# Wide GpSimd work of a hybrid backbone's mixers moved to VectorE and ScalarE

## The chip, the cores and the metric

One core of a Trainium2 chip. The metric is the device time of one execution in microseconds (us); the kernel before takes 3044.57 us, the median of three runs (3042.0 to 3048.34). TensorE (PE in the profile) multiplies matrices, VectorE (DVE) and ScalarE (ACT) work on tiles in SBUF and on PE's results in PSUM, GpSimd (POOL) works on SBUF alone, and SyncE (SP) issues the DMAs.

## The reference, cut to what matters

Two layers over 512 latent tokens and 256 context tokens of width 1024. A layer projects the modulated tokens, runs three token mixers, merges them with sigmoid gates, projects, normalises, and ends in a SwiGLU feed-forward:

```python
px = _split_in(h_x @ lp['w_in'])                       # all inputs of the mixers
p  = softmax(einsum(q, k) * MLA_SCALE); y_mla = p @ v  # 8 heads, 768 keys for latent queries
f  = lb + (1 - lb) * sigmoid(z); k = (1 - lb) * sigmoid(-z)   # gates of the recurrence, 4 heads,
S_t = diag(f_t) S_{t-1} + k_t v_t^T;  o_t = S_t^T q_t         # forwards and backwards
y_diff = rms((softmax(q1 k1) - lam * softmax(q2 k2)) @ v)     # 4 heads, rotary on q and k
m  = sum_i sigmoid(h @ w_gate[i] + b_gate[i]) * (y[i] @ w_branch[i]);  y = m @ w_o
```

Everything is fp32; the result is the latent stream.

## The kernel before, in words

All large products are made in three passes on rounded halves: a weight tile `wr` is rounded to a high part `wh` (`split_w`, line 380), the remainder is its low part `wl`, and a product is high x high + high x low + low x high (`mm3`). Activations are split likewise (`split`). Tile names in the profile are these names: `h` the modulated tokens, `k` a ring of eight large tiles of the mixers, `s` a ring of 768-wide slabs, `b` and `S` banks of PSUM, `sm` small columns.

Two kinds of work are woven into one fixed instruction order at build time. A list of jobs (projections, gates, branches, output projection, feed-forward; one weight tile each) is the filler; the mixers run as generators beside it, one after the other: attention (`mla`, 48 query tiles in layer 0 and 32 in layer 1), differential attention (`diff`), the recurrence (`hgrn`). The class `Clock` (line 93) keeps a forecast of when each engine comes free and when each tile is ready; `note` (line 199) has a duration for each kind of instruction, and for instructions of VectorE and GpSimd on SBUF it also keeps the two from overlapping (`port`, line 171). A mixer yields `At(t)`, and `weave` (line 461) then emits filler until the forecast of TensorE reaches t. A plain `yield` is a point at which the differential attention's preparation of the next head (`prep_qk`, line 1190) lets the current head go on. At run time the engines only follow their queues; a wrong forecast is a wait.

Where the weight parts are made: `split_w` gives the high part to GpSimd in the mixer stages when its forecast is more than a microsecond ahead of ScalarE's, else to ScalarE; the low part goes to the engine that the job names (`Job.eng`; "gpsimd" for the input projections, gates and branches), except that in the recurrence `lo_eng` may choose VectorE. Further GpSimd work: the softmax normalising of attention (`sB2`, line 1079, one 768- or 256-wide multiply a query tile), two rotary products a head (`prep_qk`), the rotary sum of the query projections, the scalings of the recurrence's gates in layer 1, its key sum, output gate and, on each of seven levels a head, the decay of the keys (`gen`, line 1392), and the running sum over branches (`merge_jobs`, line 1561). The recurrence's level is a chain: keys decayed, copied by ScalarE (`kcopy`), multiplied by TensorE with the queries, the queries then decayed by VectorE for the next level, and the product copied under a mask.

Small powers, the sums of the second layer's modulation weights and the affine step of the layer norms are on GpSimd too, and are not touched. Every engine call goes through the helper class `Port`, so all profile lines say L106; work is told apart by tile names and shapes.

Of the kernel before, what the change touches and what calls it, by code (L numbers as in the profile page):

```python
# [260 lines left out]
class Job:  # L261
    def __init__(self, body, load=None, n=0, eng="vector", cost=0.0):
        self.body, self.load, self.n, self.eng, self.cost = body, load, n, eng, cost
        self.raw = self.hi = self.lo = None
        self.defer = self.late = False
        self.conv = None
        self.hold = False


class Kern:  # L270
# [108 lines left out]

    def split_w(self, hi, lo, raw, eng=None):  # L380
        nc = self.nc
        if self.kp is not None and not self.inhg and self.ck.at["gpsimd"] + 1.0 < self.ck.at["scalar"]:
            nc.gpsimd.tensor_scalar(hi, raw, 1.0, 1.0, ALU.mult, ALU.mult)
        else:
            nc.scalar.copy(hi, raw)
        (eng or nc.vector).tensor_tensor(lo, raw, hi.bitcast(F32), ALU.subtract)

    def lo_eng(self, j):
        if self.inhg and j.eng == "gpsimd" and self.ck.at["vector"] < self.ck.at["gpsimd"] + 1.0:
            return self.nc.vector  # L390
        return getattr(self.nc, j.eng)

    def do_conv(self, upto):
        self.pump()
        while self.wconv < min(upto, len(self.wjobs)):
# [13 lines left out]
            j.lo = self.ck.ring("wl", 3, self.wp.tile([P, D], F32R, tag="wl", bufs=3, name=self.nm("wl")))  # L409
            self.split_w(j.hi[:, :j.n], j.lo[:, :j.n], j.raw[:, :j.n], self.lo_eng(j))  # L410
            self.rawout[j.rk] -= 1
# [506 lines left out]
    def uq_jobs(self, l):  # L918
# [4 lines left out]
        for half in range(2):  # L923
# [10 lines left out]
            def body(job, half=half):  # L934
# [3 lines left out]
                for hh in range(4):  # L938
# [59 lines left out]
    def win_jobs(self, l, names):  # L998
# [3 lines left out]
        for nmj, j in names:  # L1002
# [6 lines left out]
            def body(job, nmj=nmj, j=j, groups=groups, park=park, ctxn=ctxn):  # L1009
# [10 lines left out]
                self.done.add(f"win{l}_{nmj}{j}")  # L1020
            self.add(Job(body, self.load_fm(w, NK), 1024, "gpsimd", 24 * sum(mmcost(g[1]) for g in groups)))


    def mla(self, l):
# [54 lines left out]
        def sB2(i):  # L1079
# [91 lines left out]
    def diff(self, l):  # L1171
# [19 lines left out]
        def prep_qk(h):  # L1191
            rq, rqs, rk, rks, rv = st["raw", h]
            nc.gpsimd.tensor_tensor(rqs[:, XO:], rqs[:, XO:], rope[1][:, :TX], ALU.mult)
            yield
            nc.gpsimd.tensor_tensor(rks[:, XO:], rks[:, XO:], rope[1][:, :TX], ALU.mult)
            yield
            for rr, rs in ((rq, rqs), (rk, rks)):
                nc.vector.tensor_tensor(rr[:, XO:], rr[:, XO:], rope[0][:, :TX], ALU.mult)
                nc.vector.tensor_tensor(rr[:, XO:], rr[:, XO:], rs[:, XO:], ALU.add)
                yield  # L1200
# [13 lines left out]
            v2 = self.k6([P, 6, 256], F32R)  # L1214
            for g, m in ((0, 4), (4, 2)):
                ps = self.bank()
                for j in range(m):
# [3 lines left out]
                nc.vector.tensor_tensor(v2[:, g:g + m, P:], pv, v2[:, g:g + m, 0:P].bitcast(F32), ALU.subtract)  # L1221
                yield
            st["v", h] = v2
# [97 lines left out]
        yield At(ck.ready(*[r[:, o0:] for r in st["raw", 0]], *rope))  # L1321
        for _ in prep_qk(0):
            yield 1.0
        yield At(ck.ready(*[x[:, :, o0:] for x in st["qk", 0][:2]], st["v", 0]))
        n = len(tiles)
        per = n // 4
        pg = None
        for i in range(n + 3):
            if i < n:
# [7 lines left out]
                sB(i, 0)  # L1337
                if pg is not None:
                    next(pg, None)
                yield At(ck.freed(SS[1][:, :T]))  # L1340
                sA(i, 1)
                sB(i, 1)
                if pg is not None:
                    next(pg, None)
            elif i == n:
                sB3(i - 1)
            if 1 <= i <= n:
# [3 lines left out]
                if i < n and (i == 1 or i > 1 and i % per == 0) and h + 1 < 4:  # L1351
                    pg = prep_qk(h + 1)
                if i < n and pg is not None:
                    next(pg, None)
            if i >= 2:
# [11 lines left out]
            if i < n and i % per == per - 1 and pg is not None:  # L1367
                for _ in pg:
                    pass
                pg = None  # L1370
# [7 lines left out]
    def hgrn(self, l):  # L1378
# [13 lines left out]
        def gen(h):  # L1392
            r = st.pop(("raw", h))
            KK, QQ, TT = self.k6([P, 2, T]), self.k6([P, 2, T]), self.k6([P, 2, T])
            for d, nmj in enumerate(("ff", "fb")):
                nc.scalar.activation(TT[:, d], r[nmj][:], AF.Sigmoid)
                nc.scalar.activation(KK[:, d], r[nmj][:], AF.Sigmoid, scale=-1.0)
                if l > 0:
                    lb, l1 = self.lb[:, d, h:h + 1], self.lb1[:, d, h:h + 1]
                    nc.gpsimd.tensor_scalar(TT[:, d], TT[:, d], l1, lb, ALU.mult, ALU.add)  # L1400
                    nc.gpsimd.tensor_scalar(KK[:, d], KK[:, d], l1, 1.0, ALU.mult, ALU.mult)
            q = r["hq"]
            sq = self.slab()
# [37 lines left out]
            for lv in range(NLEV):  # L1441
# [119 lines left out]
    def merge_jobs(self, l, br, seq):  # L1561
# [30 lines left out]
        for o in range(8):  # L1592
            def gate(job, o=o):
# [8 lines left out]
            jg = Job(gate, self.load_fm(I["w_gate"][l, br][:, o * P:(o + 1) * P], NK), 1024, "gpsimd", 24 * sum(mmcost(g[1]) for g in groups))  # L1602
            gates.append(jg)

            def bran(job, o=o):
# [24 lines left out]
                if o == 7:  # L1630
                    st.clear()
                    self.done.add(f"m{l}_{seq}")
            brans.append(Job(bran, self.load_fm(I["w_branch"][l, br][:, o * P:(o + 1) * P], 4), 512, "gpsimd", 12 * sum(mmcost(g[1]) for g in groups)))
        lag = (6, 2, 8)[seq]
# [7 lines left out]
    def sweep_jobs(self, key, w, nk, tiles, lhs, use_s, needs=(), keep=2):  # L1642
# [4 lines left out]
        for k in range(nk):  # L1647
# [3 lines left out]
            def body(job, k=k):  # L1651
# [26 lines left out]
                held.clear()  # L1678
            jb = Job(body, load, 1024, "vector")
            jb.late = k >= 3  # L1680
# [369 lines left out]
```

## Time and profile before

| | |
|---|---|
| median of 3 runs | 3044.57 us |
| the profiled execution, its span | 3047.58 us, 3045.8 us |
| mean granted TensorE clock | 0.961 |
| instructions | 39105 |
| DMA | 359.14 MB, mean 118 GB/s |

The span runs from the first instruction to the last. A busy TensorE isn't TensorE at its peak, as its matmuls are pipelined; its idle time, and what ended it, says more. Idle time of an engine that nothing waits for costs nothing.

### The profile page before, as it was taken

The page shows a single profiled execution, that of the slowest core. Times are in us where ns is not written, and L with a number is a line of the kernel's source. Part 1 is how long each engine was busy: PE and PEld are TensorE (multiplying, and loading weights), DVE is VectorE, ACT ScalarE, POOL GpSimd, SP SyncE. Part 2 cuts the span into 40 slices and gives each one's busy share as a digit, 9 for nine tenths or more (in the row PEclk, how much of TensorE's full clock was granted, in tenths as well). Part 3 has the DMA queues.
Part 4 walks back from the last instruction along what each step waited for, and adds up shares of the span by engine and source line. Part 5 has one row for each costly group of instructions (what it writes and reads, how often), then busy time and mean ns, then how long its engine had stood idle before and what let it go on. Part 6 is the DMA issues. An engine that isn't in the chain of part 4 may idle for free. (4 is left out here: it accounts for less than half of the span.)

```text
span 3045.8 us, 39105 instructions
## 1 busy us (share of the span) xinstructions
PE 2772.9 (91%) x14899; PEld 2334.8 (77%) x14899; DVE 1659.1 (54%) x2398; ACT 1149.8 (38%) x2199; POOL 1001.7 (33%) x697
## 2 busy tenths in 40 slices
PE   6999987898999996999999899999899996799997
PEld 3888866777788885888888677888778775688875
DVE  4456566666773147555533765555656664622235
ACT  3544434444332124343422445443544332322222
POOL 1333332234554424333310224444336663300002
PEclk8999998999999997999999999999899997899998
DMA  6432343333333254344432354324324432433331
GB/s 212 108 102 80 111 129 93 105 115 123 115 130 116 92 178 144 121 149 132 136 128 94 120 158 130 91 77 126 102 85 149 129 110 85 140 97 97 104 131 69
DMA packets 345523, 359.14 MB, mean 118 GB/s; under 512 B 31114, under 2 KB 263044, under 8 KB 345336
## 3 DMA queue, kind: packets, MB, share of 16 engines
q1 hardware_dynamic: 343144, 351.84, 36.7%
q10 hardware_dynamic: 1680, 4.42, 0.4%
q8 instruction: 117, 1.92, 0.3%
q14 instruction: 70, 0.57, 0.1%
q0 software_dynamic: 512, 0.39, 0.1%
HBM read 298.10 MB, written 58.49 MB: 117 GB/s over the span
## 5 line engine op out<-in xcount | busy, mean ns | idle before, releaser
L106 PE MATMUL b<-h,wh 128*128 128x512 f32 (+1 forms) x5152 | 1375.2, 356 | 38.4 <-ACT h L106 16.7
L106 PEld LDWEIGHTS b<-h,wh 128*128 128x128 f32 x5152 | 909.2, 193 | 168.0 <-ACT h L106 17.9
L106 PE MATMUL b<-h,wl 128*128 128x512 f32 (+1 forms) x2576 | 907.1, 352 | 0.5 <-DVE wl L106 0.5
L106 DVE TENSOR_TENSOR wl<-wr,wh 128x1024 fp32r<-128x1024 f32 (+1 forms) x238 | 336.7, 1417 | 452.5 <-ACT wh L106 450.9
L106 PEld LDWEIGHTS b<-h,wl 128*128 128x128 f32 x2576 | 494.9, 192 | 66.0 <-DVE wl L106 1.0
L106 ACT CAST wh<-wr 128x1024 fp32r<-128x1024 f32 (+1 forms) x304 | 299.0, 988 | 417.7 <-PE b L106 325.7
L106 POOL TENSOR_TENSOR sm<-sm,mhalf 128x1 f32<-128x1 f32 (+3 forms) x80 | 56.7, 709 | 1046.1 <-DVE sm L106 1034.7
L106 POOL TENSOR_TENSOR wl<-wr,wh 128x1024 fp32r<-128x1024 f32 (+1 forms) x146 | 315.0, 2158 | 251.9 <-ACT wh L106 226.6
L106 ACT ACTIVATE s<-S,sm 128x768 f32<-128x768 f32 (+1 forms) x170 | 135.2, 796 | 383.5 <-DVE sm L106 305.9
L106 POOL TENSOR_TENSOR ln<-ln,wr 128x512 f32<-128x512 f32 x84 | 119.5, 1423 | 222.5 <-issue 161.5
L106 PE MATMUL S<-wh,ac 128*128 128x512 f32 x512 | 173.7, 404 | 17.9 <-DVE ac L106 12.8
L106 PE MATMUL b<-ident,s 128*128 128x128 f32 (+3 forms) x687 | 114.8, 282 | 70.0 <-DVE s L106 31.3
L106 DVE TENSOR_TENSOR k<-b,k 128x512 fp32r<-128x512 f32 (+1 forms) x136 | 85.1, 627 | 165.4 <-ACT k L106 165.1
L106 PE MATMUL b<-k,wh 128*128 128x512 f32 (+1 forms) x576 | 160.0, 365 | 8.6 <-ACT k L106 7.2
L106 PE MATMUL S<-k,k 96*128 96x512 f32 (+2 forms) x576 | 139.7, 345 | 28.2 <-DVE k L106 27.2
L106 DVE TENSOR_REDUCE sm<-S 128x1 f32<-128x768 f32 (+1 forms) x160 | 131.7, 837 | 47.3 <-PE S L106 47.0
L106 PE MATMUL S<-k,s 128*128 128x128 f32 (+2 forms) x704 | 132.8, 313 | 25.8 <-DVE k L106 18.3
L106 PEld LDWEIGHTS b<-ident,s 128*128 128x128 f32 (+3 forms) x687 | 82.0, 145 | 93.6 <-issue 34.0
L106 DVE TENSOR_TENSOR k<-s,k 96x768 fp32r<-96x768 f32 (+7 forms) x92 | 120.0, 1323 | 46.0 <-ACT k L106 43.2
L106 POOL TENSOR_TENSOR s<-s,s 128x512 f32<-128x512 f32 (+2 forms) x88 | 115.7, 1323 | 87.2 <-DVE s L106 63.5
L106 PEld LDWEIGHTS S<-k,k 96*128 96x128 f32 (+1 forms) x576 | 101.5, 193 | 52.6 <-DVE k L106 30.8
L106 POOL TENSOR_SCALAR wh<-wr 128x1024 fp32r<-128x1024 f32 (+1 forms) x80 | 84.5, 1063 | 164.5 <-PE b L106 148.7
(184 smaller groups left out, 4233.3 us busy)
## 6 DMA issues: line engine op xcount, KB each, us to landing
wr<-in_w_ff_dram SPq DMA_DIRECT2D x154, 512.0 KB
wr<-in_w_mod_dram SPq DMA_DIRECT2D x96, 512.0 KB
d<-s SPq DMA_DIRECT2D x88, 384.0 KB
wr<-in_w_in_dram SPq DMA_DIRECT2D x64, 512.0 KB
s<-d SPq DMA_DIRECT2D x80, 384.0 KB
wr<-in_w_gate_dram SPq DMA_DIRECT2D x48, 512.0 KB
wr<-in_w_branch_dram SPq DMA_DIRECT2D x48, 256.0 KB
wr<-in_w_o_dram SPq DMA_DIRECT2D x24, 512.0 KB
```

Source lines behind the costliest of these rows:

```text
L106: return getattr(getattr(self.clock.nc, self.eng), op)(*a, **k)
```

## The change

The engine choice goes: `split_w` always uses ScalarE for the high part and VectorE for the low part, and `lo_eng`, `Job.eng` and `Job.cost` are removed. The wide GpSimd instructions of the mixers and of the merge move to VectorE one for one, the gate scalings of the recurrence to ScalarE. In `prep_qk` the two rotary products stand before their sums, and the two transposes of the values come after an `At` for a free bank; `step` passes such an `At` on to `weave`.

```diff
-    def split_w(self, hi, lo, raw, eng=None):
+    def split_w(self, hi, lo, raw):
         nc = self.nc
-        if self.kp is not None and not self.inhg and self.ck.at["gpsimd"] + 1.0 < self.ck.at["scalar"]:
-            nc.gpsimd.tensor_scalar(hi, raw, 1.0, 1.0, ALU.mult, ALU.mult)
-        else:
-            nc.scalar.copy(hi, raw)
-        (eng or nc.vector).tensor_tensor(lo, raw, hi.bitcast(F32), ALU.subtract)
+        nc.scalar.copy(hi, raw)
+        nc.vector.tensor_tensor(lo, raw, hi.bitcast(F32), ALU.subtract)
...
-                            nc.gpsimd.tensor_tensor(qs[64:96, o:o + n], qs[64:96, o:o + n], tmp[64:96, :n], ALU.add)
+                            nc.vector.tensor_tensor(qs[64:96, o:o + n], qs[64:96, o:o + n], tmp[64:96, :n], ALU.add)
...
-            nc.gpsimd.tensor_scalar(pr[:, :n], pr[:, :n], rs[:], 1.0, ALU.mult, ALU.mult)
+            nc.vector.tensor_scalar(pr[:, :n], pr[:, :n], rs[:], None, ALU.mult)
...
-            nc.gpsimd.tensor_tensor(rqs[:, XO:], rqs[:, XO:], rope[1][:, :TX], ALU.mult)
-            yield
-            nc.gpsimd.tensor_tensor(rks[:, XO:], rks[:, XO:], rope[1][:, :TX], ALU.mult)
-            yield
             for rr, rs in ((rq, rqs), (rk, rks)):
+                nc.vector.tensor_tensor(rs[:, XO:], rs[:, XO:], rope[1][:, :TX], ALU.mult)
+                yield
                 nc.vector.tensor_tensor(rr[:, XO:], rr[:, XO:], rope[0][:, :TX], ALU.mult)
...
             for g, m in ((0, 4), (4, 2)):
+                yield At(max(ck.next("b", 4), ck.ready(rv)))
                 ps = self.bank()
...
+        def step(pg):
+            r = next(pg, None) if pg is not None else None
+            if r is not None:
+                yield r
+                next(pg, None)
...
-                    nc.gpsimd.tensor_scalar(TT[:, d], TT[:, d], l1, lb, ALU.mult, ALU.add)
-                    nc.gpsimd.tensor_scalar(KK[:, d], KK[:, d], l1, 1.0, ALU.mult, ALU.mult)
+                    nc.scalar.activation(TT[:, d], TT[:, d], AF.Identity, scale=l1, bias=lb)
+                    nc.scalar.activation(KK[:, d], KK[:, d], AF.Identity, scale=l1)
...
-            nc.gpsimd.tensor_tensor(sq[:, o0:], KK[:, 0, o0:], KK[:, 1, o0:], ALU.add)
+            nc.vector.tensor_tensor(sq[:, o0:], KK[:, 0, o0:], KK[:, 1, o0:], ALU.add)
...
-            nc.gpsimd.tensor_tensor(g[:, o0:], g[:, o0:], sg[:, o0:], ALU.mult)
+            nc.vector.tensor_tensor(g[:, o0:], g[:, o0:], sg[:, o0:], ALU.mult)
...
-                nc.gpsimd.tensor_tensor(kv, kv, tk, ALU.mult)
+                nc.vector.tensor_tensor(kv, kv, tk, ALU.mult)
...
-                        nc.gpsimd.tensor_tensor(sg[:, oo:oo + n], sg[:, oo:oo + n], mo[:, oo:oo + n], ALU.add)
+                        nc.vector.tensor_tensor(sg[:, oo:oo + n], sg[:, oo:oo + n], mo[:, oo:oo + n], ALU.add)
```

## Rows read from the trace of the kernel before

**Rows 1.** The page: busy us, share of the span, instructions of each engine.
```profile
PE 2772.9 (91%) x14899; PEld 2334.8 (77%) x14899; DVE 1659.1 (54%) x2398; ACT 1149.8 (38%) x2199; POOL 1001.7 (33%) x697
```
**Rows 2.** Windows: length, PE, PEld, DVE, ACT, POOL busy, granted clock, DMA.
```profile
126.00:384.00 258.00, 248.28 (x1539) 216.12 (x1538) 146.14 (x272) 119.28 (x271) 101.56 (x87) 0.99 0.35 108
384.00:684.00 300.00, 249.92 (x1420) 208.54 (x1419) 196.09 (x337) 130.37 (x306) 91.66 (x73) 0.93 0.36 110
684.00:912.00 228.00, 210.23 (x1326) 182.47 (x1325) 167.96 (x202) 93.14 (x163) 112.67 (x55) 0.98 0.38 123
912.00:1076.00 164.00, 161.77 (x971) 143.13 (x971) 42.97 (x66) 33.96 (x60) 77.96 (x59) 1.00 0.33 105
...
1880.00:2084.00 204.00, 198.31 (x1250) 177.35 (x1250) 98.44 (x177) 83.03 (x179) 82.38 (x63) 1.00 0.34 100
2084.00:2270.00 186.00, 162.35 (x908) 139.69 (x907) 120.91 (x207) 87.46 (x199) 66.85 (x47) 0.94 0.31 93
2270.00:2510.00 240.00, 228.03 (x1187) 190.71 (x1187) 158.00 (x197) 92.11 (x170) 146.79 (x89) 0.99 0.42 132
2510.00:2590.00 80.00, 52.46 (x229) 41.49 (x229) 36.80 (x65) 17.89 (x36) 31.79 (x22) 0.79 0.26 87
```
**Rows 3.** Waits of PE, 384 to 684: total us, times, longest us.
```profile
PE b L106 <- DVE s L106: 16.8, 6, 7.3
PE b L106 <- DVE sm L106: 10.4, 6, 2.9
PE b L106 <- ACT s L106: 7.0, 7, 2.4
PE S L106 <- ACT s L106: 6.8, 9, 1.2
PE b L106 <- DVE k L106: 4.9, 2, 2.7
PE S L106 <- DVE k L106: 4.0, 1, 4.0
```
**Rows 4.** Timeline, 393 to 403: start us, us, instruction [idle before, releaser].
```profile
397.14 2.65 POOL L106 TENSOR_TENSOR wl<-wr,wh 128x1024 fp32r<-128x1024 f32 x1
397.52 3.09 DVE L106 SCALAR_TENSOR_TENSOR s<-s,k 64x768 fp32r<-64x768 f32 x1
...
400.63 0.95 DVE L106 TENSOR_TENSOR k<-s,k 64x768 fp32r<-64x768 f32 x1
...
402.10 0.69 PE L106 MATMUL b<-ident,s 128*128 128x128 f32 x2 [7.35 <-DVE s L106]
```
**Rows 5.** Tile wl: duration ns min/median/max, first and last start, forms.
```profile
L106 DVE TENSOR_TENSOR wl<-wr,wh x238: 693/1226/3399, 6.8 to 3009.2; 128x1024 fp32r<-128x1024 f32 x117, 128x512 fp32r<-128x512 f32 x2
...
L106 POOL TENSOR_TENSOR wl<-wr,wh x146: 1262/2387/3471, 50.2 to 2581.2; 128x1024 fp32r<-128x1024 f32 x104, 128x512 fp32r<-128x512 f32 x42
```
**Rows 6.** The page's costliest groups: busy us, mean ns, idle before and releaser.
```profile
L106 DVE TENSOR_TENSOR wl<-wr,wh 128x1024 fp32r<-128x1024 f32 (+1 forms) x238 | 336.7, 1417 | 452.5 <-ACT wh L106 450.9
L106 ACT CAST wh<-wr 128x1024 fp32r<-128x1024 f32 (+1 forms) x304 | 299.0, 988 | 417.7 <-PE b L106 325.7
L106 POOL TENSOR_TENSOR s<-s,s 128x512 f32<-128x512 f32 (+2 forms) x88 | 115.7, 1323 | 87.2 <-DVE s L106 63.5
L106 POOL TENSOR_SCALAR wh<-wr 128x1024 fp32r<-128x1024 f32 (+1 forms) x80 | 84.5, 1063 | 164.5 <-PE b L106 148.7
```
**Rows 7.** Groups by line, GpSimd: the keys' decay and the normalising.
```profile
L106 POOL TENSOR_TENSOR k<-k,k 128x768 f32<-128x768 f32 x32 | 70.0, 2186 | 16.3 <-ACT s L106 8.5 <-DVE k L106 5.6 <-PE S L106 2.1
...
L106 POOL TENSOR_SCALAR s<-s,sm 128x768 f32<-128x768 f32 (+1 forms) x80 | 65.7, 822 | 203.3 <-DVE sm L106 121.7 <-issue 33.9 <-ACT s L106 16.9
```
**Rows 8.** Tile ln on DVE: a multiply by columns, min/median/max ns.
```profile
L106 DVE TENSOR_SCALAR ln<-ln,sm,sm x16: 803/807/2911, 1137.7 to 2654.1; 128x1024 f32<-128x1024 f32 x16
```
**Rows 9.** Waits of PE, 126 to 384.
```profile
PE S L106 <- DVE k L106: 8.2, 8, 1.9
```
**Rows 10.** Waits of PE, 2510 to 2590.
```profile
PE S L106 <- DVE k L106: 6.4, 2, 5.5
```

More of the change, by code (lines that the diff above doesn't have):

```diff
@@ L261, with __init__ @@
 class Job:
-    def __init__(self, body, load=None, n=0, eng="vector", cost=0.0):
-        self.body, self.load, self.n, self.eng, self.cost = body, load, n, eng, cost
+    def __init__(self, body, load=None, n=0):
+        self.body, self.load, self.n = body, load, n
         self.raw = self.hi = self.lo = None
@@ L378, in pump @@
             self.wload += 1
-    def split_w(self, hi, lo, raw, eng=None):
+    def split_w(self, hi, lo, raw):
         nc = self.nc
-        if self.kp is not None and not self.inhg and self.ck.at["gpsimd"] + 1.0 < self.ck.at["scalar"]:
-            nc.gpsimd.tensor_scalar(hi, raw, 1.0, 1.0, ALU.mult, ALU.mult)
-        else:
-            nc.scalar.copy(hi, raw)
-        (eng or nc.vector).tensor_tensor(lo, raw, hi.bitcast(F32), ALU.subtract)
[L388 to L391, printed above, removed]
+        nc.scalar.copy(hi, raw)
+        nc.vector.tensor_tensor(lo, raw, hi.bitcast(F32), ALU.subtract)
     def do_conv(self, upto):
@@ L409, in do_conv @@
             j.lo = self.ck.ring("wl", 3, self.wp.tile([P, D], F32R, tag="wl", bufs=3, name=self.nm("wl")))
-            self.split_w(j.hi[:, :j.n], j.lo[:, :j.n], j.raw[:, :j.n], self.lo_eng(j))
+            self.split_w(j.hi[:, :j.n], j.lo[:, :j.n], j.raw[:, :j.n])
             self.rawout[j.rk] -= 1
@@ L1020, in body @@
                 self.done.add(f"win{l}_{nmj}{j}")
-            self.add(Job(body, self.load_fm(w, NK), 1024, "gpsimd", 24 * sum(mmcost(g[1]) for g in groups)))
+            self.add(Job(body, self.load_fm(w, NK), 1024))
     def mla(self, l):
@@ L1221, in prep_qk @@
                 nc.vector.tensor_tensor(v2[:, g:g + m, P:], pv, v2[:, g:g + m, 0:P].bitcast(F32), ALU.subtract)
-                yield
+                if g == 0:
+                    yield
             st["v", h] = v2
@@ L1321, in diff @@
         yield At(ck.ready(*[r[:, o0:] for r in st["raw", 0]], *rope))
-        for _ in prep_qk(0):
-            yield 1.0
+        for r in prep_qk(0):
+            yield r or 1.0
         yield At(ck.ready(*[x[:, :, o0:] for x in st["qk", 0][:2]], st["v", 0]))
+        def step(pg):
[3 more added lines that the diff above has]
+                next(pg, None)
         n = len(tiles)
@@ L1337, in diff @@
                 sB(i, 0)
-                if pg is not None:
-                    next(pg, None)
+                yield from step(pg)
                 yield At(ck.freed(SS[1][:, :T]))
@@ L1342, in diff @@
                 sB(i, 1)
-                if pg is not None:
-                    next(pg, None)
+                yield from step(pg)
             elif i == n:
@@ L1352, in diff @@
                     pg = prep_qk(h + 1)
-                if i < n and pg is not None:
-                    next(pg, None)
+                yield from step(pg)
             if i >= 2:
@@ L1367, in diff @@
             if i < n and i % per == per - 1 and pg is not None:
-                for _ in pg:
-                    pass
+                for r in pg:
+                    if r is not None:
+                        yield r
                 pg = None
@@ L1601, in gate @@
                     yield c
-            jg = Job(gate, self.load_fm(I["w_gate"][l, br][:, o * P:(o + 1) * P], NK), 1024, "gpsimd", 24 * sum(mmcost(g[1]) for g in groups))
+            jg = Job(gate, self.load_fm(I["w_gate"][l, br][:, o * P:(o + 1) * P], NK), 1024)
             gates.append(jg)
@@ L1632, in bran @@
                     self.done.add(f"m{l}_{seq}")
-            brans.append(Job(bran, self.load_fm(I["w_branch"][l, br][:, o * P:(o + 1) * P], 4), 512, "gpsimd", 12 * sum(mmcost(g[1]) for g in groups)))
+            brans.append(Job(bran, self.load_fm(I["w_branch"][l, br][:, o * P:(o + 1) * P], 4), 512))
         lag = (6, 2, 8)[seq]
@@ L1678, in body @@
                 held.clear()
-            jb = Job(body, load, 1024, "vector")
+            jb = Job(body, load, 1024)
             jb.late = k >= 3
```

## The prediction

> **What bounds the kernel now.** Read the busy shares first: TensorE (PE) is busy 91% of the span, VectorE (DVE) 54%, ScalarE (ACT) 38%, GpSimd (POOL) 33% [rows 1]. A mean over stages with different limits says little, so next the windows, cut where the weight loads and parked results on SyncE change stage [rows 2]. Per row, window length less PE busy is what PE lost: attention in layer 0 (126 to 384) 9.7 us, differential attention (384 to 684) 50.1, the recurrence (684 to 912) 17.8, the rest of the merge (912 to 1076) 2.2; in layer 1 5.7 (1880 to 2084), 23.7 (2084 to 2270), 12.0 (2270 to 2510) and 27.5 (2510 to 2590). So PE's work bounds the attention stages and the merge, and waits bound the differential stages and the end of the layer 1 mixers. In those the granted clock is down too: 0.93, 0.94 and 0.79, against 0.99 to 1.00 elsewhere. As the work list is emitted in one fixed order and the layer 0 merge still runs at 99% PE busy, PE time saved earlier in layer 0 is saved at the end.
>
> Third, who ended PE's waits in the worst window [rows 3]: DVE 36.1 us (16.8 + 10.4 + 4.9 + 4.0), ACT 13.8 (7.0 + 6.8). Fourth, one such wait in order of time [rows 4]: a GpSimd low part from 397.14 to 399.79, a VectorE instruction over 64x768 that takes 3.09 us beside it, and PE standing 7.35 us until a VectorE copy queued behind that has run. The next VectorE instruction of the same width took 0.95 us at 400.63.
>
> Fifth, the price list. The same low part (1024 wide) takes VectorE 1.226 us in the median and 3.399 at worst, GpSimd 2.387 in the median [rows 5]: worst is about one GpSimd instruction more than median. The 238 on VectorE mean 1.417 [rows 6], so some 238 x 0.19 = 45 us of them are waiting for GpSimd. That is the bottleneck the change touches: not VectorE's load but what GpSimd does to it.
>
> The Trainium skill (SBUF — State Buffer, "Who interferes with whom") says that a VectorE instruction with two SBUF inputs and a GpSimd instruction that reads SBUF hold a shared port in turn, the later one blocked for the whole of the earlier. By that rule, and 3.399 against 1.226 agrees, every wide instruction that leaves GpSimd also takes a blocker away from VectorE. Were the two engines independent, the same move would only lengthen VectorE's queue, and rival A would be the outcome.
>
> **The change part by part.** (1) Low parts, 146 off GpSimd, 104 of 1024 and 42 of 512 [rows 5]: at 1.226 and 0.693 (the shortest VectorE one) 128 + 29 = 157 us go to VectorE, 315 leave GpSimd. (2) High parts, 80 off GpSimd at 1.06 us (84.5 us) to ScalarE at 0.99 [rows 6]: +79 us there; 16 scalings of the recurrence's gates go with them, at about 0.95 (three quarters of the 1024 cast as the lower end, 0.74; GpSimd's own whole microsecond as the upper): +15. (3) Softmax normalising, 80, 0.82 on GpSimd [rows 7]. VectorE's price at 768 isn't in the trace; a 1024-wide multiply by a column took 0.807 [rows 8], so 0.6 from it by width, 0.81 at most; I take 0.65 for the 64 wide and 0.3 for the 16 narrow ones: 47 us. (4) Adds and rotary products, 88, 1.32 on GpSimd [rows 6], 128x512 for the most part; half a 1.226 low part and a little: 0.65 each, 57 us. (5) The recurrence's key decay, 56 (32 are in [rows 7] at 2.19). Strided and broadcast, so nothing shows it on VectorE; by width three quarters of 1.226 is 0.92, above it at most GpSimd's 2.19. I take 1.0, nearest to the plain rows: 56 us, at the upper end 123. With 8 key sums (6 us) VectorE gets some 323 us, and gives back at least the 45 of waiting: at most 1659 + 278 = 1937 of 3046, 64%.
>
> Where do these lie? In the attention stages VectorE goes from 146 of 258 us and 98 of 204 [rows 2] up by a little over half of what GpSimd does there, to about 0.72 and 0.65 of the window. PE's only VectorE waits there are short: 8.2 us in 8 [rows 9]. A tile has 258 / 48 = 5.4 us; its normalising now stands in VectorE's queue between the reciprocal (which waits for ScalarE's exponential) and the next tile's maximum, so maximum, exponential and products of the next tile come 0.65 us later. The filler matmuls cover that; without them it would be 80 x 0.65 = 52 us. I charge a doubling of those short waits, rounded: **+10 us**.
>
> Differential attention, layer 0: the 13.8 us that ACT ends stay, ScalarE having more to do. Of DVE's 36.1 three quarters go, because low parts and casts on GpSimd stand beside the long VectorE instructions, and because the value transposes now wait, by forecast, for their bank behind filler instead of in PE's queue (the 7.35 us wait in [rows 4] is one of these; the edit adds no instruction): **-27**, bounds 0 and -50. The low clock is (1 - 0.93) x 300 = 21 us of lost full-speed work at most; half returns with the waits: **-10**, bounds 0 and -21. Layer 1, same reasoning on 23.7 us: **-12**, bounds 0 and -24, and half of 0.06 x 186 = 11 for the clock: **-5**. Recurrence, layer 0: 17.8 us, **-8**. What is late next in these stages is ScalarE: 1 us casts in front of exponentials.
>
> Recurrence and end of layer 1: 12.0 + 27.5 us. At 2510 the filler is used up and the last head's chain stands alone; 5.5 us there is one wait for a VectorE product [rows 10]. With GpSimd at 147 of 240 us in that window [rows 2] each level of the chain waits for a 2.19 us instruction and what it blocks. A decay of 1.0 us shortens a level by a microsecond or more, 28 levels, so heads use less filler and some is left for the last one. The decay's wait for ScalarE's key copy now stands in VectorE's queue before two query products and a masked copy; they fill more time than the copy takes and wait for PE anyway, so I charge nothing; uncovered it would be some 0.9 us a level, 25 us. Half returns: **-20**, bounds +25 and -39.
>
> The merge windows have room (VectorE 43 of 164 us) and take their share at nothing; with that cover gone it would be at most half of GpSimd's 78 us there, 39. No DMA moves; GpSimd's queue keeps the small powers, which no longer stand behind 2.4 us instructions.
>
> Sum: -27 - 10 - 12 - 5 - 8 - 20 + 10 = -72. The profiled execution took 3047.6 us (its span 3045.8 and 1.8 around it), so 2975.6; it is 3.0 above the median of the runs, so on their scale **2973**.
>
> **The rivals.** A, VectorE becomes PE's queue, slower. In the attention stages VectorE rises to about 0.7 of the window, the level that differential attention has now (196 of 300), where PE loses 16.7% against 3.3%. If attention follows, 462 us x 13.4% = +62, and a clock of 0.93 there another 0.06 x 462 = +28: instead of +10, so 3047.6 - 82 + 90 = 3056, or 3053. It decides when maxima and low parts of the attention stages come late by more than the filler between two tiles. Against it: the recurrence in layer 0 has VectorE at 168 of 228 and loses only 8%; load alone does not make the waits.
> The Trainium skill (Perfetto Trace Analysis, "Optimizing Scalar/DVE Operations") advises the other direction when VectorE is saturated, offloading to ScalarE or even GpSimd, while warning that between VectorE and GpSimd it might not help. No window of [rows 2] has VectorE above 0.74, so I weigh it as rival A and no more.
>
> B, the waits belong to the fixed order, not to GpSimd: the planner spends its filler as before and stalls reappear behind ScalarE. Then a quarter of the 82 comes, little is lost: about 3047.6 - 20 + 5 - 3 = 3030. For it: ACT ends 13.8 us of waits already. Against: the 3.09 us instruction beside GpSimd.
>
> C, nearly all waits in the five mixer windows go (50 + 24 + 18 + 12 + 28 = 131) with the clock (32): 3047.6 - 163 + 10 - 3 = 2892 at the very end, some 2915 as a case. For it: each saved wait also keeps the clock up.
>
> **How the numbers follow.** Forecast 0.58 (2935 to 3020), C 0.12, B 0.14, A 0.16. A measurement of this kernel can tell about 0.2%, 6 us, from no change. The forecast, C and most of B are faster: 0.58 + 0.12 + 0.10 = 0.80; the rest of B and a little of A within 0.2%: 0.07; slower 0.13. The range leaves out the far end of C and most of A: 2920 to 3050.
>
> **What would show it.** VectorE low parts at 1.23 us with a maximum near it, none on GpSimd; PE's loss in the first differential window from 50 to about 23 us with a clock of 0.96 or more; the wait after the last head shorter by half; attention windows no more than 10 us worse together. The prediction is wrong if attention loses more than 80 us more, or if PE's waits in the differential windows stay and only change their releaser to ACT.

## The result and the profile after

The changed kernel takes 2991.5 us, the median of four runs (2988.58 to 2997.48), against 3046.45 for the kernel before beside it: a ratio of 0.9823 with an interval of 0.9803 to 0.9844, a gain of 55 us where 72 were forecast. The profiled execution took 2997.48 us (span 2995.7, mean granted clock 0.964). The span is 50.1 us shorter than before, and the first weight loads of two stages say where. The output projection of layer 0 starts loading at 1064.5 instead of 1074.6 (-10). From there to the first query weight of layer 1 it is 741.5 us instead of 747.0 (-6), from that to the output projection of layer 1 719.2 instead of 753.3 (-34), and from there to the end 470.5 instead of 470.9. By the terms of the forecast, with the attention's charge halved between the layers, it should have been -40 in the mixers of layer 0 and -32 in those of layer 1. The second came; the first did not. The 6 us between the two stood in no term of the forecast.

The page's busy line, which answers to [rows 1], and its two costliest groups, which answer to [rows 6]:
```profile
PE 2759.8 (92%) x14899; PEld 2327.7 (78%) x14899; DVE 1729.5 (58%) x2776; ACT 1271.7 (42%) x2321; POOL 273.0 (9%) x223
...
L106 DVE TENSOR_TENSOR wl<-wr,wh 128x1024 fp32r<-128x1024 f32 (+1 forms) x384 | 478.1, 1250 | 603.3 <-ACT wh L106 602.4
L106 ACT CAST wh<-wr 128x1024 fp32r<-128x1024 f32 (+1 forms) x384 | 379.8, 995 | 419.1 <-PE b L106 326.8
```
VectorE has 378 instructions more, 323 us of work by the prediction's price list, and is busy only 70 us longer: by that list 253 us of its busy time before were not its own work. The trace gives nearly the same without a price list: the kinds of VectorE instruction that stand in both kernels (same tiles, same shape) took 241 us longer before. One such kind, a product of two tiles in SBUF in the recurrence of layer 1, before and after (count, busy us, mean ns):
```profile
L106 DVE TENSOR_TENSOR k<-k,k 128x256 f32<-128x256 f32 x32 | 41.0, 1320 | 11.1 <-PE S L106 11.0
...
L106 DVE TENSOR_TENSOR k<-k,k 128x256 f32<-128x256 f32 x32 | 12.0, 417 | 0.6 <-PE S L106 0.5
```
All 384 low parts are on VectorE. Their mean fell from 1417 to 1250 ns, but half of that is the many half as wide ones that came with them: at the full width of 1024 it went from 1414 to 1331 ns.

Eight windows, cut at the same changes of stage as [rows 2] (length, busy time of PE, PEld, DVE, ACT and POOL, granted clock, DMA share, GB/s):
```profile
126.00:419.00 293.00, 282.17 (x1737) 244.36 (x1736) 192.78 (x355) 145.69 (x301) 0.00 (x0) 1.00 0.38 114
419.00:726.00 307.00, 255.97 (x1489) 215.27 (x1487) 182.08 (x363) 183.66 (x355) 12.49 (x23) 0.94 0.35 107
726.00:925.00 199.00, 186.90 (x1164) 163.56 (x1165) 153.37 (x256) 81.28 (x148) 4.54 (x4) 0.93 0.39 128
925.00:1066.00 141.00, 139.27 (x847) 123.80 (x846) 59.90 (x99) 37.00 (x65) 1.32 (x1) 1.00 0.33 103
1864.00:2080.00 216.00, 211.73 (x1300) 186.85 (x1299) 135.96 (x241) 102.21 (x206) 0.00 (x0) 1.00 0.34 101
2080.00:2270.00 190.00, 174.43 (x980) 151.15 (x979) 123.50 (x227) 111.30 (x222) 7.07 (x13) 0.96 0.35 106
2270.00:2465.00 195.00, 186.95 (x1005) 157.91 (x1003) 134.56 (x253) 94.70 (x172) 4.67 (x6) 0.98 0.45 142
2465.00:2540.00 75.00, 65.77 (x326) 53.13 (x326) 52.82 (x94) 25.67 (x48) 1.01 (x1) 0.95 0.33 108
```
Length less PE busy is again what PE lost. In the order of the rows it was 9.7, 50.1, 17.8, 2.2, 5.7, 23.7, 12.0 and 27.5 us before; it is 10.8, 51.0, 12.1, 1.7, 4.3, 15.6, 8.1 and 9.2 now. Layer 1 lost 69 us and loses 37. Layer 0 lost 80 and still loses 76, 51 of them in the differential attention as before, at a clock of 0.94 against 0.93. And the attention of layer 0 has grown: its window is 293 us instead of 258, with 1737 matmuls in it instead of 1539 and PE as busy as before. The time is not idle, it is filler that was used up there.

PE's waits in the differential window of layer 0 (419 to 726), which answer to [rows 3] (total us, times, longest us):
```profile
PE b L106 <- ACT s L106: 21.0, 9, 4.8
PE b L106 <- DVE k L106: 11.4, 6, 3.0
PE b L106 <- DVE s L106: 8.6, 4, 4.4
PE b L106 <- DVE sm L106: 6.4, 3, 4.9
PE S L106 <- ACT s L106: 0.9, 1, 0.9
```
ScalarE ended 13.8 us of them before and ends 21.9 now; VectorE ended 36.1 and ends 26.4. One group of ScalarE's has grown (the groups of after by form; busy us and mean ns, then its idle time before):
```profile
L106 ACT ACT_TABLE_LOAD x33 | 42.3, 1283 | 1.3 <-PEq L2034 0.7
```
There were 7 of these, 9.0 us, in the kernel before. ScalarE's timeline from 600 us (start us, us, instruction) shows how one comes about, and PE's line beside it the wait that it falls into (in the run below without Sigmoid the wait at this place of the order is still 3.4 us, so the load is not the whole of it):
```profile
600.16 0.90 ACT L106 ACTIVATE s<-S,sm 128x768 f32<-128x768 f32 x1 [1.28 <-DVE sm L106]
600.97 0.19 ACT L106 ACTIVATION_READ_ACCUMULATOR s<-S,sm 128x1 f32 x1
601.06 1.03 ACT L106 CAST wh<-wr 128x1024 fp32r<-128x1024 f32 x1
602.11 1.28 ACT L106 ACT_TABLE_LOAD   x1
603.40 0.69 ACT L106 ACTIVATE s<-b,colv 128x512 f32<-128x512 f32 x1
```
```profile
604.14 0.48 PE L106 MATMUL b<-ident,s 128*128 128x128 f32 x1 [4.77 <-ACT s L106]
```
At 600.16 stands the Exp of a softmax, at 603.40 the Sigmoid of a merge gate, and between them the table is loaded; the next Exp needs it loaded back. Before, the first such switch was at 671, after the last maximum of the stage (667.4). Now it is at 602, the last maximum is at 715, and 20 of the 33 loads lie between 602 and 713: the gates, which are filler, are reached while the differential attention still takes exponentials.

The low parts on their own (tile wl: duration min/median/max in ns), to be held against [rows 5]:
```profile
L106 DVE TENSOR_TENSOR wl<-wr,wh x384: 671/1226/3395, 6.8 to 2959.1; 128x1024 fp32r<-128x1024 f32 x167, 128x512 fp32r<-128x512 f32 x25
```
The maximum has stayed, but outside the mixers, beside the layer norms' and the modulation's GpSimd work, which was not touched. In the mixers and the merge of layer 0 (126 to 1076 before, to 1066 now) the wide ones, before and after, are:
```profile
L106 DVE TENSOR_TENSOR wl<-wr,wh 128x1024 fp32r<-128x1024 f32 x35 | 51.2, 1462 | 2.3 <-POOL wh L106 1.3 <-ACT wh L106 0.9
...
L106 DVE TENSOR_TENSOR wl<-wr,wh 128x1024 fp32r<-128x1024 f32 x86 | 103.8, 1222 | 81.6 <-ACT wh L106 81.1
```
None of the 86 takes more than 1.24 us.

### The profile page after: what moved, and what is told of

Read it like the earlier page. It is cut to its first block, busy times and chain, and to the rows that moved or that the text cites. A ratio compares the mean times of both kernels' runs of the same rounds, so it can differ in the third digit from the quotient of the medians.

```text
span 2995.7 us, 38612 instructions
## 1 busy us (share of the span) xinstructions
PE 2759.8 (92%) x14899; PEld 2327.7 (78%) x14899; DVE 1729.5 (58%) x2776; ACT 1271.7 (42%) x2321; POOL 273.0 (9%) x223
## 5 line engine op out<-in xcount | busy, mean ns | idle before, releaser
L106 DVE TENSOR_TENSOR wl<-wr,wh 128x1024 fp32r<-128x1024 f32 (+1 forms) x384 | 478.1, 1250 | 603.3 <-ACT wh L106 602.4
L106 ACT CAST wh<-wr 128x1024 fp32r<-128x1024 f32 (+1 forms) x384 | 379.8, 995 | 419.1 <-PE b L106 326.8
L106 PE MATMUL S<-k,k 96*128 96x512 f32 (+2 forms) x576 | 137.3, 341 | 12.6 <-DVE k L106 12.1
L106 PEld LDWEIGHTS S<-wh,ac 128*128 128x128 f32 x512 | 97.2, 192 | 45.4 <-DVE ac L106 16.8
L106 PEld LDWEIGHTS b<-k,wh 128*128 128x128 f32 x576 | 103.5, 195 | 30.3 <-ACT k L106 11.7
L106 PE MATMUL S<-k,s 128*128 128x128 f32 (+2 forms) x704 | 123.9, 298 | 1.3 <-ACT s L106 0.9
L106 ACT ACTIVATE wr<-wr,cact 128x512 f32<-128x512 f32 x84 | 59.9, 723 | 143.2 <-DVE ln L106 116.9
L106 ACT ACTIVATE ac<-b 128x512 f32<-128x512 f32 (+1 forms) x67 | 34.9, 520 | 191.7 <-PE b L106 191.6
```

The lines of the kernel that those rows point to most:

```text
L106: return getattr(getattr(self.clock.nc, self.eng), op)(*a, **k)
```

## The experiments

All times are medians, and the ratios are to runs of the kernel before on the same chip. The medians of the kernel before lie between 3043.33 and 3047.11 us, so between two changed kernels a few us are better read from the ratios (0.001 is 3 us). Except where the text says that an order is kept, an edit makes the planner lay the order anew. Theory 1: GpSimd's wide instructions held VectorE up, and taking them away is the gain, less what the new order spoils. Rival 1: the gain is the order that the planner lays out from the new forecast, whatever the engines do.

**Engines without the order.** The order of the kernel before is kept on every queue, and only at the call are the wide GpSimd instructions handed to the other engines:
```diff
+            if self.eng == "gpsimd" and op in ("tensor_tensor", "tensor_scalar") and a[0].free_size() >= 128:
+                if name.startswith("wh"):
+                    return nc.scalar.copy(a[0], a[1])
+                if name.startswith(("wl", "s", "k")):
+                    if op == "tensor_tensor":
+                        return nc.vector.tensor_tensor(*a, **k)
...
```


> The kernel before with its emission order and forecast kept, only the engines of the change: every wide GpSimd instruction of the mixers is issued on VectorE or ScalarE at the same place. Theory 1: VectorE is no longer blocked, table loads stay at 7, layer 0 attention stays near 202 us; PE's loss in the first differential window falls from 50 to 25 or less; time 2950 to 2985, at or below the changed kernel's. Rival 1 (the gain comes from the new order and its truer forecast, not from unblocking): 3025 to 3050.


It took 3029.27 us, ratio 0.9944 [0.9929, 0.9958]: 18 us faster than before, and rival 1's number. Its windows over attention, differential attention and the end of layer 1 (columns as above):
```profile
126.00:404.00 278.00, 253.69 (x1521) 216.83 (x1520) 180.19 (x340) 132.79 (x284) 0.00 (x0) 0.98 0.33 99
404.00:690.00 286.00, 245.56 (x1401) 204.97 (x1400) 178.63 (x362) 150.78 (x327) 13.03 (x24) 0.94 0.37 115
...
2497.00:2571.00 74.00, 53.09 (x238) 44.02 (x238) 49.98 (x91) 19.90 (x40) 1.01 (x1) 0.77 0.30 97
```
and the first line of PE's waits in the attention of layer 0 (helper lines are L119 in this kernel):
```profile
PE S L119 <- DVE k L119: 15.6, 10, 3.7
```
VectorE's instructions are as short here as in the changed kernel (the kinds that both have differ by 2 us in all), so the blocking is gone and only the order differs. The differential window loses 40 us instead of 50, so the engines do gain there. But attention loses 24 us instead of 9.7, probably as the normalising on VectorE has no place in the old forecast, and the end of layer 1 still loses 21 at a clock of 0.77: there the faster chains brought little while the order laid the same filler beside them. Theory 1 in its simple form falls; so does "the order alone", as the next run shows.

**The new order with GpSimd busy.** Every queue of the changed kernel is as it was, and GpSimd reads the high parts of the mixer and merge weights in instructions that compute nothing:
```diff
+            if j.side:
+                for o in range(0, min(j.n, 768), 256):
+                    hv = j.hi[:, o:o + 256].bitcast(F32)
+                    self.ck.nc.gpsimd.tensor_tensor(self.scr[:], hv, hv, ALU.subtract)
```


> The changed kernel in the same order with the suspected cost put back alone: after each of the 146 weight splits that before had its low part on GpSimd, GpSimd subtracts the high part from itself in pieces of 256 into a scratch tile (three for a 1024 wide part, two for a 512 wide), some 2.2 us, that nobody reads. Theory 1: VectorE's low parts and products are blocked, mean of a low part from 1.25 to 1.4 us or more, PE waits on DVE return, time 3015 to 3045. Rival 1 (order, not blocking): 2987 to 2996.


It took 3029.19 us, 0.9946 [0.993, 0.9963], 38 us more than the changed kernel. Two groups, low parts and the added instructions (busy us, mean ns):
```profile
L106 DVE TENSOR_TENSOR wl<-wr,wh 128x1024 fp32r<-128x1024 f32 (+1 forms) x384 | 495.5, 1295 | 598.4 <-ACT wh L106 597.1
...
L407 POOL TENSOR_TENSOR scr<-wh 128x256 f32<-128x256 f32 x432 | 425.5, 985 | 1119.1 <-ACT wh L106 1097.3
```
GpSimd's 425 us are on nobody's path by their result, and the low parts take 17 us longer in all. That is less than expected (a mean of 1.4 us or more); in the mixers and the merge of layer 0 the wide ones take 1331 ns against 1222. All of VectorE, with the same 2776 instructions, is busy 61 us longer (1729.5 us in the changed kernel):
```profile
PE 2764.2 (91%) x14899; PEld 2324.4 (77%) x14899; DVE 1790.1 (59%) x2776; ACT 1271.9 (42%) x2321; POOL 698.8 (23%) x655
```
The added instructions also hold a weight's high part until they have read it, but a buffer that comes free late for this explains little: ScalarE's idle time before its casts ended with one of them once, 3.1 us. The Trainium skill (SBUF — State Buffer, "Who interferes with whom") has a VectorE instruction with two SBUF inputs and a GpSimd one that reads SBUF exclude each other for a whole instruction; the longer low parts agree.

So engines alone give 18 us, the new order with GpSimd kept busy 18, and both together 55: either is worth most where the other is there. The useless work is a stand-in only: it stretched VectorE's instructions by 61 us, the kernel before by 241.

**One part at a time on the kernel before.** Low parts alone (high parts, normalising, adds and recurrence stay):
```diff
-        return getattr(self.nc, j.eng)
+        return self.nc.vector
```


> The kernel before with one part of the change: all low parts of the weights on VectorE, the rest of GpSimd's work left (the planner lays its order anew). It takes 315 of the some 650 us that the change takes off GpSimd. Theory 1 (gain goes with the GpSimd time taken away from beside VectorE): about half of 55, 3010 to 3030. Rival 1 (the order decides, each part can go either way): anything from 2990 to 3055.


3000.54 us, 0.9852 [0.9836, 0.9869]: 45 us of gain, more than half of the whole and 10 us beyond theory 1's range; the order has a part in it that this run can't separate. The differential stage of layer 0 loses 32.9 us at a clock of 0.95, the attention stage keeps its 202 us (first to last maximum). The recurrence alone (decay, key sum, gate product to VectorE, scalings to ScalarE):
```diff
-                nc.gpsimd.tensor_tensor(kv, kv, tk, ALU.mult)
+                nc.vector.tensor_tensor(kv, kv, tk, ALU.mult)
...
```


> The kernel before with one part of the change: the recurrence's key decay, key sum and output gate on VectorE and its gate scalings on ScalarE. Theory 1: each of the seven levels a head is shorter, heads go from 65 to 55 us or less, filler is left for the last head of layer 1, whose end loses 15 to 25 us less: 3015 to 3030. Rival (low parts on GpSimd still block the levels): 3035 to 3047.


3015.98 us, 0.99 [0.9886, 0.9915], 29 us of gain, as expected: -28 had been forecast for the recurrence of both layers. A head takes 54 us in layer 0 where it took 62 to 66. Added up the two parts give 74 us, more than the whole change: if parts add up, some other part of it costs about 20.

**The table loads.** In the changed kernel the gates take Identity in place of Sigmoid:
```diff
-  nc.scalar.activation(sg[:, oo:oo + n], ps[:, :n], AF.Sigmoid, bias=...)
+  nc.scalar.activation(sg[:, oo:oo + n], ps[:, :n], AF.Identity, bias=...)
```


> The changed kernel in the same order, with the merge gates' Sigmoid replaced by Identity (the gates are left out of the computation; same instruction, shape and forecast). It prices the 26 extra table loads of ScalarE alone: 26 x 1.28 = 33 us on ScalarE. Theory 1 (the loads stand in PE's way in differential attention, where ScalarE ends most of the new waits): loads back at 7, time 2965 to 2980. Rival 2 (the loads are hidden, the loss in that stage comes from the order itself): 2985 to 2993.


2975.96 us, 0.9769 [0.9754, 0.9783]: 15.5 us less. The group and the differential window of layer 0:
```profile
L106 ACT ACT_TABLE_LOAD x7 | 9.0, 1283 | 0.8 <-PEq L2034 0.7
```
```profile
416.00:713.00 297.00, 255.13 (x1488) 215.85 (x1486) 182.05 (x362) 156.53 (x334) 12.41 (x23) 0.94 0.37 111
```
The 26 extra loads are gone, and the window loses 41.9 us, not the 23 of the forecast. What ScalarE ends of its waits is 14.2 us, as before the change (13.8), and the largest line of them is
```profile
PE b L106 <- ACT s L106: 13.0, 6, 3.4
```
VectorE still ends 25.2. So the loads are a part of what went wrong, about 9 of the 51.0 us of this stage. That 33 us of loads cost the kernel only 15.5 fits ScalarE's timeline of the changed kernel: of the 20 loads between 602 and 713 us ten lead back to Exp, and after nine of these ScalarE still waits 1.2 to 2.3 us before its exponential; after the ten that lead to a Sigmoid it goes on 0.01 us later. The Trainium skill (ScalarE: Activation LUTs, "What ACT_TABLE_LOAD costs") gives 1283 ns for a load and about 2.66 us for a switch with its drain; the trace has the 1283, but no drain beside it (ScalarE's next instruction often starts 0.01 us after the load, as at 603.40). By an estimate from the skill's figure 26 switches would be 69 us of ScalarE; here they cost 0.6 us of the kernel's time each.

**The attention's normalising.** In the changed kernel it goes back to GpSimd, all else kept:
```diff
-            nc.vector.tensor_scalar(pr[:, :n], pr[:, :n], rs[:], None, ALU.mult)
+            nc.gpsimd.tensor_scalar(pr[:, :n], pr[:, :n], rs[:], 1.0, ALU.mult, ALU.mult)
```


> The changed kernel with one part undone: attention's softmax normalising is on GpSimd again. Theory 1 (the new order eats filler): on VectorE the normalising stands in the forecast's chain from one tile's exponential to the next tile's maximum, so layer 0 attention takes 239 us from first to last maximum instead of 202 and uses up filler; Sigmoid gates then run beside the Exp of differential attention, with 33 table loads on ScalarE instead of 7. Undone, attention is back at 200 to 215 us, the loads at 7 to 10, and the time falls to 2960 to 2985. Rival 2 (table loads and filler order are hidden, only blocking by GpSimd counts): 80 GpSimd instructions block VectorE again, 2990 to 3005.


2956.45 us, 0.9706 [0.9691, 0.9721]: 35 us less than the changed kernel. Its first three windows, its table loads, and PE's first wait from 381 to 685:
```profile
126.00:381.00 255.00, 246.15 (x1523) 214.47 (x1523) 156.29 (x294) 133.69 (x285) 36.88 (x48) 0.99 0.36 108
381.00:685.00 304.00, 272.41 (x1609) 228.74 (x1608) 187.50 (x373) 175.86 (x354) 13.24 (x24) 0.98 0.39 120
685.00:881.00 196.00, 185.92 (x1222) 164.43 (x1221) 152.74 (x250) 84.31 (x151) 3.99 (x3) 0.99 0.41 133
```
```profile
L106 ACT ACT_TABLE_LOAD x17 | 21.8, 1283 | 1.0 <-PEq L2034 0.7
```
```profile
PE b L106 <- ACT s L106: 15.8, 8, 4.7
```
Attention is back at 255 us and 1523 matmuls (203 us from first to last maximum), and the filler that it had eaten lies in the later stages again: the differential attention now has 1609 matmuls instead of 1489, loses 31.6 us and runs at 0.98. Layer 0 is 38 us shorter, layer 1 unchanged (717.8 us of mixers against 719.2). Here the forecast for layer 0 is met and passed: -49 for its mixers. The time is a little below the expected range, and the table loads are 17, not 7 to 10, so theory 1 had their number wrong.

Rival 2 fell because these GpSimd instructions blocked nothing. VectorE's busy time is 1683.6 us, 45.9 less than in the changed kernel, and the 80 normalisings took it 45.4: all its other work takes as long as without them. Of the 80 on GpSimd 65 run beside one of VectorE's maxima, which reads PSUM, 13 beside nothing, and two beside an instruction of VectorE with two inputs.

How the one instruction does that is in VectorE's own queue. Changed kernel, 300 to 301.4, layer 0's attention (start us, us):
```profile
300.25 0.15 DVE L106 RECIPROCAL sm<-sm 128x1 f32<-128x1 f32 x1
300.43 0.62 DVE L106 TENSOR_SCALAR s<-s,sm 128x768 f32<-128x768 f32 x1
300.97 0.42 DVE L106 TENSOR_REDUCE sm<-S 128x1 f32<-128x256 f32 x1
```
The kernel before, one reciprocal:
```profile
276.91 0.15 DVE L106 RECIPROCAL sm<-sm 128x1 f32<-128x1 f32 x1
276.98 0.93 DVE L106 TENSOR_REDUCE sm<-S 128x1 f32<-128x768 f32 x1
```
The next tile's maximum stands behind the normalising, and its exponential behind the maximum. The 48 tiles of layer 0, first to last maximum, took 202 us and take 239, 0.78 us more for each step from tile to tile, and the planner puts filler into these.

Two more ways to take it out of that chain. On ScalarE:
```diff
-            nc.vector.tensor_scalar(pr[:, :n], pr[:, :n], rs[:], None, ALU.mult)
+            nc.scalar.activation(pr[:, :n], pr[:, :n], AF.Identity, scale=rs[:])
```


> The changed kernel with attention's normalising on ScalarE: neither GpSimd blocks nor VectorE queues. Theory 1 (it is VectorE's queue between exponential and next maximum that makes layer 0 attention 239 us and lets gates run into the Exp stage): attention 205 to 220 us, table loads under 20, time 2955 to 2975. Rival 3 (any in-order engine of that chain costs the same; GpSimd is good there because it is idle): attention 230 us or more, 2985 to 3000.


2960.86 us, 0.9734 [0.9718, 0.975], 31 us of gain by the medians and 27 by the ratios: attention 217 us, 19 loads, 36.3 us lost in the differential stage at 0.98. On VectorE, but behind the next maximum:
```diff
-            if 1 <= i <= n:
-                sB2(i - 1)
             if i < n:
                 sB(i)
+            if 1 <= i <= n:
+                sB2(i - 1)
```


> The changed kernel with the normalising of a tile emitted behind the next tile's maximum and exponential, still on VectorE. Theory 1: the forecast's chain is shorter by one 0.62 us multiply a tile, so layer 0 attention falls from 239 us by 10 to 35, table loads from 33 to under 20, time 2965 to 2985. Rival 2: nothing is blocked in either, so 2987 to 2996.


2975.24 us, 0.9767 [0.9752, 0.9781], 16 us less than the changed kernel, with attention at 197 us and 9 loads. So the place in the queue is what lengthens the attention, though not by itself what costs all of the 35 us. The differential stage loses 42.2 us here at a clock of 0.92, with the loads gone and no more gates before its last maximum than in the kernel before (18): neither can be the whole of its waits, and why this order has them is open.

**High parts and the wait for a bank.** The run with the normalising on GpSimd, and the high parts chosen by forecast as before:
```diff
+        if self.kp is not None and not self.inhg and self.ck.at["gpsimd"] + 1.0 < self.ck.at["scalar"]:
+            nc.gpsimd.tensor_scalar(hi, raw, 1.0, 1.0, ALU.mult, ALU.mult)
+        else:
+            nc.scalar.copy(hi, raw)
```


> The kernel with the normalising back on GpSimd (2956 us), and the high parts too chosen as in the kernel before (GpSimd when ScalarE's forecast is behind). It tells what the move of the high parts brought. Theory 1 (casts on GpSimd block VectorE, on ScalarE they are cheap): slower by 5 to 20, 2961 to 2976. Rival (ScalarE is what is late next in differential attention): faster, 2940 to 2955.


2960.4 us, 0.9724 [0.9709, 0.9738], against 0.9706 [0.9691, 0.9721]: the intervals overlap, so moving the high parts is worth 4 us or nothing, and the time lies between the two ranges expected. The changed kernel without the At in front of the value transposes:
```diff
             for g, m in ((0, 4), (4, 2)):
-                yield At(max(ck.next("b", 4), ck.ready(rv)))
                 ps = self.bank()
...
-                if g == 0:
-                    yield
+                yield
```


> The changed kernel without the forecast wait ahead of the value transposes of differential attention. Theory 1 (a few long bank waits of PE return): 2 to 4 us more for each of some 3 heads a layer, 2995 to 3010. Rival (the wait only moves filler): within 5 us of 2991, either side.


2985.17 us, 0.98 [0.9785, 0.9814]: the wait by forecast cost 6 us by the medians, if anything, where the prediction had counted it for a gain. Theory 1 expected a loss without it; none came. Without it and with the normalising on GpSimd:


> The kernel with the normalising back on GpSimd, and without the forecast wait ahead of the value transposes. If the 6 us that the wait cost in the changed kernel is the wait's own, 2948 to 2954; if it came from the table loads it happened to shift (33 to 25), there is nothing to gain here: 2953 to 2962.


2945.08 us (2944.78 to 2946.32), 0.9675 [0.9661, 0.969]: the fastest of all, 98 us under the kernel before and 46 under the changed one, and better than either range. Page line and the four windows of layer 0:
```profile
PE 2740.9 (93%) x14899; PEld 2316.5 (79%) x14899; DVE 1684.7 (57%) x2696; ACT 1252.8 (43%) x2307; POOL 340.6 (12%) x303
```
```profile
126.00:380.00 254.00, 245.16 (x1528) 213.66 (x1528) 156.82 (x294) 134.27 (x287) 36.76 (x48) 1.00 0.36 109
380.00:678.00 298.00, 267.39 (x1575) 224.81 (x1574) 185.13 (x368) 172.09 (x348) 12.64 (x23) 0.97 0.40 122
678.00:875.00 197.00, 186.83 (x1207) 164.21 (x1207) 155.89 (x254) 86.89 (x155) 4.54 (x4) 0.98 0.39 130
875.00:1028.00 153.00, 151.27 (x918) 134.33 (x917) 63.48 (x105) 39.71 (x69) 1.32 (x1) 1.00 0.34 105
```
Its layer 0 is no shorter than with the At (output projection at 1027.3 against 1026.0); the 11 us come in layer 1. And with the normalising on ScalarE and no At:


> The kernel with the normalising on ScalarE (2961 us), without the forecast wait ahead of the value transposes: a third pair for the wait's own price. If the wait costs some 6 to 11 us by itself, 2948 to 2956, and level with the best so far (2945); if its price hangs on what else is on the engines, 2958 to 2966.


2960.31 us, 0.9712 [0.9696, 0.9729], by the median no less than with it. By the medians the wait cost 6, 11 and 0.5 us in three orders, by the ratios 7, 9 and 7, and only the middle pair has intervals that don't overlap: a small cost is likely, and whether it depends on the order is not shown.

## Why the prediction was right, and which step of it failed

**The mechanism** was right as far as GpSimd holding VectorE up goes: low parts cost VectorE the forecast 1.226 us, and GpSimd work without any use beside the new order cost 38 us. It is not the whole: freeing VectorE in the old order brought 18 of the 55 us. The prices held too (groups of after by form; busy us, mean ns):
```profile
L106 DVE TENSOR_SCALAR s<-s,sm 128x768 f32<-128x768 f32 x64 | 39.7, 620 | 2.3
...
L106 DVE TENSOR_TENSOR k<-k,k 128x768 f32<-128x768 f32 x32 | 36.0, 1126 | 0.0
...
L106 DVE TENSOR_TENSOR k<-k,s 128x768 f32<-128x768 f32 x24 | 22.8, 951 | 0.0
...
L106 DVE TENSOR_TENSOR s<-s,s 128x512 f32<-128x512 f32 x84 | 57.5, 688 | 7.1 <-DMA s<-d 5.5
```
Normalising was put at 0.65 and takes 0.62; the key decay at 1.0 and takes 0.95 to 1.13; the adds at 0.65 and take 0.69. VectorE was bounded by 64% and is at 58%: the 45 us that it was to get back at least were some 240 to 250.

**Layer 1** came out by the terms: its differential attention -12, and -8 measured in PE's loss; its clock -5, from 0.94 to 0.96 over 190 us -4; recurrence and end -20, and 39.5 less 17.3 is -22. The recurrence of layer 0 was put at -8, and its waits fell by 6, but its clock fell from 0.98 to 0.93, which is 9 us of full-speed work (0.07 x 199 less 0.02 x 228): PE is busy only 7.1 us from 719 to 736, and the clock is at its lower level from 719 to 740. With the normalising on GpSimd it is at 0.99. The wait on the last head's chain, 27.5 us at a clock of 0.79 in [rows 2], is 9.2 at 0.95, shorter by more than half.

**The step that failed** is "-27" and "-10" for the differential attention of layer 0. It loses 51.0 us, at 0.94: nothing came. What failed in it is the sentence on attention before it, "The filler matmuls cover that; without them it would be 80 x 0.65 = 52 us". They do cover it: PE's loss in attention rose by 1.1 us in layer 0 and fell by 1.4 in layer 1, so the +10 was too much if anything. But the 0.65 us was paid in filler: the tiles took 37 us longer in layer 0 and 7 in layer 1 (170 to 177 us), 44 of the 52. The charge looked at PE's idle time, and cover isn't free in a fixed order whose filler is a stock. With 34 us of it spent early, the differential attention drew on later jobs, 31 gates before its last maximum instead of 18, and Sigmoid met Exp. With the instruction back on GpSimd the stage loses 31.6 us at 0.98: -18 and, over 304 us, -15 against -27 and -10, which is the forecast's sum within 5 us. That run can't say how much of the 35 us is table loads, how much the lack of filler; the gates without Sigmoid put all 26 extra loads at 15.5, and at 9 of the 51.0 us that the stage loses. That the rest is the lack of filler is argued, not shown: with the normalising behind the next maximum the filler is back and the stage still loses 42.2 us.

By the prediction's own signs layer 1 and the last head are right and the first differential window is not: its waits stayed at 51 us, and a part of them changed their releaser to ScalarE. The whole came out at 55 of 72 us although 30 of the 40 us forecast for the mixers of layer 0 didn't come: layer 1 gave 34 against 32, 6 us came between the layers that no term had, and the profiled execution from which these are read is 6 us above the median. To that extent it is luck that the time lies so near the forecast.

**The wait for a bank** was counted among the reasons of the -27, and without it the kernel is faster by 0.5 to 11 us by the medians. It was no gain in any order tried.

**Rivals.** A, VectorE as PE's queue in attention, did not happen: VectorE is at 66% of the layer 0 window and 63% of the layer 1 one, and in the first PE's waits that it ends are 5.0 us against 9.6. (The prediction's 0.72 and 0.65 don't follow from its own words: half of GpSimd's 101.56 and 82.38 us put on top gives 0.76 and 0.68. The windows grew, so the shares came out lower.) Yet the instruction that A was about did the harm, by lengthening a chain, not by filling a queue. B said that stalls would reappear behind ScalarE under the planner's order; in layer 0's differential attention that is seen in part (ScalarE ends 21.9 of 51.0 us), in layer 1 not. C was out of reach by the change, though the best order, 2945, lies about halfway from the forecast to its 2915.

**What stays open**: why the differential stage of layer 0 keeps 30 us of waits or more in every order tried, and how much of the gain of a single part is the part and how much the order that the planner happened to lay for it.

## What to carry to other kernels

When an instruction changes its engine, write down what then stands behind it in the new queue: a multiply of 0.62 us in front of the next tile's maximum, once a tile, came to some 35 us, and the idle GpSimd was the better place for it. Look too at what runs beside an instruction before calling it a blocker: the normalisings stood beside maxima over PSUM and held nothing up. Where an order is fixed ahead from a forecast, a lengthened chain shows up not as idle time in its own stage but as filler missing in a later one, so compare instruction counts by stage and not only waits. And let the order be laid out anew with the new durations: engines alone gave 18 us here, engines and order 55.

## What the runs showed of the hardware

A table load on ScalarE is 1.283 us, and 26 of them, between Exp and Sigmoid, cost 15.5 us of the kernel's time and not their 33. GpSimd instructions whose result nobody waits for, 425 us of them, made VectorE's same instructions 61 us longer and cost the kernel 38 us. Beside 80 one-input GpSimd instructions that met VectorE's maxima over PSUM, VectorE's other work took no longer. The same width of two-input work takes VectorE 1.226 and GpSimd 2.387 us (1024 wide). The 48 normalisings of an attention stage take GpSimd 36.9 us in all, and with them there PE lost 8.9 us in that stage against 10.8 with them on VectorE.
